# One encoder layer on one core: the state-space model's input operand built in its transposed layout

## The chip, the core and the metric

The kernel runs on one core of a Trainium2 chip. The metric is the device time of one execution in microseconds (us). The matrix engine is TensorE (PE in the rows; PEld is its weight load), the others are VectorE (DVE), ScalarE (ACT), GpSimd (POOL) and SyncE (SP), which issues every DMA of this kernel. The instructions of all engines are written out in a fixed order when the kernel is built; at run time each engine works through its own list and waits on semaphores.

## The reference

One layer of a streaming encoder, in float32: x is (512, 1024), 256 memory tokens, model width 1024.

```
z = rms_norm(x) @ w_in            # -> u (1024), q, k, v (1024 each), gates (2048)
a = S5(u): per group g of 64 (16 channels, 64 complex states):
    lam_bar = exp(lam * dt);  b_bar = (lam_bar - 1) / lam * b
    state_l = lam_bar * state_(l-1) + b_bar @ u_l          # over 512 positions
    y_l = Re(c @ state_l) + d * u_l
    a = gelu(y); a = a * sigmoid(a @ w_glu + b_glu); a = a @ w_ssm_proj
b = differential attention (8 heads, rotary, chunk-causal) @ w_da_proj
x = x + rms_norm((g_a * a + g_b * b) @ w_mix_out)
x = x + rms_norm(cross_attention(x, mem));  x = x + rms_norm(relu(x @ w_ff1)^2 @ w_ff2)
```

## The kernel before

**Wide products.** Every float32 product with a weight is done as three products in the reduced format fp32r: operand and weight are split into a high and a low part, and high*low, low*high and high*high are added up in PSUM. A weight unit is 128 x 1024 values. A DMA brings it (`wraw`, two buffers), ScalarE makes the high part (`whi`), VectorE or POOL the low one (`wlo`, four buffers). A projection (`proj`, L443) takes one unit and one PSUM bank and runs 24 products of 512 columns. The eight banks of PSUM are shared out by class with `quotas`: in the stretch of interest three for projections ("mm"), two for transposes and small products ("t"), two for attention scores ("s"), one for attention outputs ("o") (`QUO`, L71).

**Order.** The kernel is written as coroutines. `spawn` gives each a rank (the R values, L60), and a planner (`step`, L248) keeps for each engine the time up to which it is filled, by its own cost figures. It always lets the coroutine of lowest rank go on whose next instruction is ready: an instruction of another engine is written when TensorE's planned time has reached the time at which its inputs are ready, and at which its engine is filled for no more than `SLACK` (L56, 700 ns) ahead (`when`, L244). A DMA is written `SLACK` ahead of the time at which its source is ready (`load`, L228). The projections come in a fixed sequence from the `filler`, at the worst rank: first v, then for each head the u, q and k products and some gate products (`ULEAD` and `GL`, the number of gates behind each head). `self.X` writes an operation to VectorE or POOL, whichever the planner has done earlier; `self.Y` is VectorE alone while `YX` is 0. `PORT` says for each phase whether the planner keeps operations of the two that use a common port apart.

**Attention.** q and k of a head are rotated (`rope`, L938) in tiles `ropeB` and `ropeA`, of which there is one each, and moved by six DMAs a product into the operands. Four blocks a head compute scores, softmax, the difference of the two maps, a transpose and the output; `PBUF` (3) is the number of softmax buffers.

**State-space model.** The 64 groups are worked off in eight steps m of eight groups, four pairs each. Positions are cut into 64 chunks of 8; the powers of lam_bar are made once (`ssm_tables`, L664): `L` to the power 8, in float32, and `Lw` = powers times (lam_bar - 1)/lam, kept in SBUF; `L`, its imaginary part and the negative of that also go to DRAM (`scr_L`). Then for each m:

- `ssm_pre` (L764), rank 0.1: loads b and c (`bc`) and rows of the powers (`L2`); E = Lw x b (complex, six operations of 512 columns); copies E's first step into `bb`, block by block (four ScalarE copies); C = c x powers (three operations of 1024 columns and a copy).
- `ssm_mid` (L803): transposes E by eight TensorE transposes into two banks, and two ScalarE copies bring them to `ET`; the product of `bb` and C gives the kernel of short distances, which goes through DRAM (`sk`) and comes back as eight DMAs of 16 rows (`Dt`, one buffer).
- `ssm_main` (L847): waits for u of this m, loads it (`u2`), takes `ET` x u (state product, 32 small products), rotates back and forth around a scan over the chunks (`rr`, z, `S["s"]`), and adds C x state and `Dt` x u (64 small products) to y. GELU and four DMAs to DRAM follow.

The tiles `E`, `ET`, `bb`, the temporaries and z are cuts of one tile `ga`. After the eighth m, `gelu` (L1077) reads y back and splits it, and the GLU products begin; each needs all eight. The merge of the branches waits for the GLU and for all heads.

Of the kernel before, what the change touches and what calls it, by code (L numbers as in the profile page):

```python
# [26 lines left out]
KB = 8  # L27
# [28 lines left out]
SLACK = 700.0  # L56
PORT = (1,1,1,1,0,0,0,0)
PACE = 2.5
PEM = 500.0
R_TAB, R_PRE, R_ROT, R_MID, R_MAIN, R_U, R_ATT, R_BLK, R_ROPE, R_GATE, R_W = 1, 0.1, -0.55, -0.3, -0.6, -0.5, -0.45, 0, -0.45, 0, -0.3  # L60
# [3 lines left out]
YX = 0  # L64
# [38 lines left out]
class Kern:  # L103
# [464 lines left out]
    def consts(self):  # L568
# [12 lines left out]
        self.scr_L = [self.dram.tile([P, NPAIR, T + 1], F32, name=f"scr_L{i}") for i in range(3)]  # L581
        self.scr_g = [self.dram.tile([P, SEQ], F32, name=f"scr_g{m}") for m in range(16)]
# [65 lines left out]
    def ssm_alloc(self, pool):  # L648
        S = self.S
        S["Lw_re"], S["Lw_im"] = (self.t(pool, [P, NPAIR, T], x) for x in ("Lw_re", "Lw_im"))  # L650
        S["qa_re"], S["qa_im"], S["qb_re"], S["qb_im"] = (self.t(pool, [P, NPAIR, T], x) for x in ("qa_re", "qa_im", "qb_re", "qb_im"))
        S["r8"] = self.t(pool, [P, NPAIR], "r8")
        S["bb"] = self.t(pool, [P, 4, 2, 2, 16], "bb")
        S["s"] = self.t(pool, [P, 4, 2, NC], "st")
        S["K"] = self.t(pool, [P, NSLOT, 16], "kev")
        for k in ("bb", "s", "K"):
            self.nc.gpsimd.memset(S[k], 0.0)
# [6 lines left out]
    def ssm_tables(self):  # L664
# [49 lines left out]
        nL = self.tmp(N, T + 1)  # L714
        yield from self.A.activation(out=nL, in_=L_im[:, :N], func=AF.Copy, scale=-1.0)
        for i, x in enumerate((L_re[:, :N], L_im[:, :N], nL)):
            yield from self.load(self.scr_L[i], x)
# [10 lines left out]
        for h in range(2):  # L728
            c = slice(4 * h, 4 * h + 4)
            yield from self.cmul4(v, S["Lw_re"][:, :, c], S["Lw_im"][:, :, c], L_re[:, :N, c], L_im[:, :N, c],  # L730
                                  w_re.unsqueeze(2).broadcast_to((P, N, 4)), w_im.unsqueeze(2).broadcast_to((P, N, 4)),
                                  *[x[:, :N] for x in tt])
# [31 lines left out]
    def ssm_pre(self, pool, m):  # L764

        v, g, S = self.V, self.G, self.S
        bc = yield from self.alloc(pool, [P, 384], "bc")
        yield from self.load(bc, self.a["bc"][m])
        L2 = yield from self.alloc(pool, [P, 2, 2, 36], "L2")
        for i, h, x in ((0, 0, 0), (0, 1, 0), (1, 0, 2), (1, 1, 1)):  # L770
            yield from self.load(L2[64 * h:64 * h + 64, i],
                                 self.scr_L[x][:, 4 * m:4 * m + 4].rearrange("(a s) j t -> s a (j t)", a=2))
        sl = slice(4 * m, 4 * m + 4)
        b_re, b_im = (bc[:, 64 * i:64 * i + 64].rearrange("p (j h) -> p j h", j=4) for i in range(2))
        L_re, L_im = S["Lw_re"][:, sl].unsqueeze(3), S["Lw_im"][:, sl].unsqueeze(3)
        t1, t2 = (x.rearrange("p (j t h) -> p j t h", j=4, h=16) for x in S["ct"])
        yield from self.lock("E")
        E_re, E_im = (x.rearrange("p (j t h) -> p j t h", j=4, h=16) for x in S["E"])
        sh = (P, 4, T, 16)
        yield from self.cmul(S["eng_e"], E_re, E_im, L_re.broadcast_to(sh), L_im.broadcast_to(sh),  # L780
                             b_re.unsqueeze(2).broadcast_to(sh), b_im.unsqueeze(2).broadcast_to(sh), t1, t2)
        yield from self.lock("bb")
        for par in range(2):
            s = slice(64 * par, 64 * par + 64)
# [3 lines left out]
        sh = (P, 8, T, 16)  # L788
        x, y = (bc[:, 128 * i:128 * i + 128].rearrange("p (j h) -> p j h", j=8) for i in (1, 2))
# [472 lines left out]
    def build(self):  # L1262
# [116 lines left out]
        def rot_all():  # L1379
            for m in range(8):  # L1380
                yield from self.ssm_rot(sp, m)
# [299 lines left out]
```

## Time and profile before

| | us |
|---|---|
| median of 3 runs | 1077.8 (1073.1 to 1080.18) |
| profiled execution | 1077.05 |
| its span, first to last instruction | 1075.0 |
| TensorE busy | 1057.1 (98%) |
| VectorE busy | 645.1 (60%) |
| ScalarE busy | 525.9 (49%) |
| POOL busy | 71.8 (7%) |

The busy time of TensorE is modelled and a product overlaps the next, so a wide product shows 390 ns where the next begins some 227 ns after it. Starts are therefore what to compare. The stages are: v, tables and normalisation (to about 60 us), state-space model and attention (to about 362 us), GLU (to 416 us), merge and output projection, cross-attention (to about 730 us), MLP.

### The profile page before, as it was taken

The page shows a single profiled execution, that of the slowest core. Times are in us where ns is not written, and L with a number is a line of the kernel's source. Part 1 is how long each engine was busy: PE and PEld are TensorE (multiplying, and loading weights), DVE is VectorE, ACT ScalarE, POOL GpSimd, SP SyncE. Part 2 cuts the span into 40 slices and gives each one's busy share as a digit, 9 for nine tenths or more (in the row PEclk, how much of TensorE's full clock was granted, in tenths as well). Part 3 has the DMA queues.
Part 4 walks back from the last instruction along what each step waited for, and adds up shares of the span by engine and source line. Part 5 has one row for each costly group of instructions (what it writes and reads, how often), then busy time and mean ns, then how long its engine had stood idle before and what let it go on. Part 6 is the DMA issues. An engine that isn't in the chain of part 4 may idle for free.

```text
span 1075.0 us, 15625 instructions
## 1 busy us (share of the span) xinstructions
PE 1057.1 (98%) x5854; PEld 884.0 (82%) x5854; DVE 645.1 (60%) x1125; ACT 525.9 (49%) x1051; POOL 71.8 (7%) x83
## 2 busy tenths in 40 slices
PE   9999999999999999999999999999999999999997
PEld 7887788888887788888898888889888888888885
DVE  6898879988877774444487555475442223443234
ACT  6757567767766774222455444354342214433131
POOL 1020201010200000000022000010000000000001
PEclk9999999999999999999999999999999999999999
DMA  8458377585774954444565512323332333332322
GB/s 301 138 150 216 106 172 202 137 201 141 188 169 127 215 147 136 143 142 141 193 212 159 157 59 59 119 79 118 98 97 92 94 95 96 97 97 98 98 78 79
DMA packets 96042, 146.38 MB, mean 136 GB/s; under 512 B 45664, under 2 KB 57440, under 8 KB 95968
## 3 DMA queue, kind: packets, MB, share of 16 engines
q1 hardware_dynamic: 95968, 145.39, 46.5%
q8 instruction: 46, 0.75, 0.3%
q14 instruction: 28, 0.23, 0.1%
HBM read 120.87 MB, written 11.91 MB: 124 GB/s over the span
## 4 chain that ended last, share of the span: by engine, by line
PE 87%; DVE 5%; ACT 3%; DMA 2%; issue 2%; SPq 1%; POOL 0%; POOLq 0%; DVEq 0%; ACTq 0%
PE ps L368 85%; PE ps L377 2%; DVE wlo L98 1%; DVE ga L98 1%; ACT ropeB L98 1%; SPq L219 1%; DMA xr<-in_x_dram 1%; DMA q<-ropeB 1%; DMA scr_u<-ev 0%; DMA Dt<-sk 0%; DVE hTl L98 0%; ACT p L98 0%; ACT whi L98 0%; POOL ropeB L98 0%; DVE ropeA L98 0%
## 5 line engine op out<-in xcount | busy, mean ns | idle before, releaser
L98 DVE TENSOR_TENSOR wlo<-wraw,whi 128x1024 fp32r<-128x1024 f32 (+1 forms) x180 | 217.7, 1209 | 294.2 <-ACT whi L98 291.2
L98 ACT CAST whi<-wraw 128x1024 fp32r<-128x1024 f32 (+1 forms) x180 | 185.9, 1033 | 285.7 <-PE ps L368 257.3
L368 PE MATMUL ps<-hTl,whi 128*128 128x512 f32 (+1 forms) x736 | 286.9, 390 | 0.4 <-DVE sm L98 0.4
L368 PE MATMUL ps<-hTh,wlo 128*128 128x512 f32 (+1 forms) x736 | 280.7, 381 | 0.0
L368 PE MATMUL ps<-hTh,whi 128*128 128x512 f32 (+1 forms) x736 | 280.7, 381 | 0.0
L368 PEld LDWEIGHTS ps<-hTh,whi 128*128 128x128 f32 x736 | 138.7, 188 | 27.2
L368 PEld LDWEIGHTS ps<-hTl,whi 128*128 128x128 f32 x736 | 138.9, 189 | 25.1 <-issue 1.2
L368 PEld LDWEIGHTS ps<-hTh,wlo 128*128 128x128 f32 x736 | 139.0, 189 | 23.4
L368 PE MATMUL ps<-whi,vy 128*128 128x512 f32 x384 | 123.6, 389 | 0.0
L368 PE MATMUL ps<-whi,g2l 128*128 128x512 f32 x256 | 99.7, 389 | 0.0
L368 PE MATMUL ps<-wlo,vy 128*128 128x512 f32 x224 | 87.7, 392 | 0.0
L368 PEld LDWEIGHTS ps<-whi,vy 128*128 128x128 f32 x384 | 72.1, 188 | 15.0
L368 PE MATMUL ps<-wlo,g2h 128*128 128x512 f32 x192 | 74.9, 390 | 0.0
L368 PE MATMUL ps<-whi,g2h 128*128 128x512 f32 x192 | 74.7, 389 | 0.0
L368 PE MATMUL ps<-vy,whi 128*128 128x512 f32 (+1 forms) x256 | 65.4, 338 | 0.0
L368 PEld LDWEIGHTS ps<-whi,g2l 128*128 128x128 f32 x256 | 48.1, 188 | 9.8
L98 POOL TENSOR_TENSOR sm<-sm,mhalf 128x1 f32<-128x1 f32 (+1 forms) x28 | 26.3, 942 | 364.7 <-DVE sm L98 358.8
L368 PEld LDWEIGHTS ps<-wlo,vy 128*128 128x128 f32 x224 | 42.1, 188 | 8.5
L368 PEld LDWEIGHTS ps<-vy,whi 128*128 128x128 f32 x256 | 44.4, 189 | 5.0
L98 DVE TENSOR_REDUCE sm<-ps 128x1 f32<-128x256 f32 (+3 forms) x80 | 37.0, 472 | 15.2 <-PE ps L368 15.0
L368 PE MATMUL ps<-vy,wlo 128*128 128x512 f32 (+1 forms) x128 | 43.0, 336 | 0.0
L368 PEld LDWEIGHTS ps<-wlo,g2h 128*128 128x128 f32 x192 | 36.0, 188 | 7.6
(220 smaller groups left out, 1514.5 us busy)
## 6 DMA issues: line engine op xcount, KB each, us to landing
wraw<-in_wall_dram SPq DMA_DIRECT2D x172, 512.0 KB, 3.6
xr<-in_x_dram SPq DMA_DIRECT2D x8, 512.0 KB, 5.5
q<-ropeB SPq DMA_DIRECT2D x32, 128.0 KB, 3.4
scr_g<-gt SPq DMA_DIRECT2D x16, 256.0 KB, 4.4
Dt<-sk SPq DMA_DIRECT2D x64, 64.0 KB, 3.3
gl<-scr_g SPq DMA_DIRECT2D x16, 256.0 KB, 3.8
mg<-scr_y SPq DMA_DIRECT2D x12, 256.0 KB, 4.5
gain<-in_gains_dram SPq DMA_DIRECT2D x5, 512.0 KB, 5.4
```

What stands on the lines that cost most here:

```text
L98: getattr(k.eng[best], "copy" if (best, m) == ("ACT", "tensor_copy") else m)(**kw)
L219: self.nc.sync.dma_start(out=out, in_=in_)
L368: self.nc.tensor.matmul(out, lhsT=lhsT, rhs=rhs, start=start, stop=stop, **kw)
L377: self.nc.tensor.transpose(out, in_, self.ident)
```

## The change

E is no longer built in the layout of C and transposed. In the tables, the powers are transposed once (four TensorE transposes for all m) and stored in DRAM (`scr_W`); a new coroutine `ssm_in`, rank 0.1, loads for each m the rows of powers, each broadcast to 16 partitions by a DMA (`Lt`, eight DMAs), and b in the transposed layout from the host (`bt`), and computes `ET` directly with four operations. The factor (lam_bar - 1)/lam, which was in E, is now in C: `scr_L` holds Lw, its negative real part and its negative imaginary part, and C takes nine steps at once (1152 columns) without the copy. `bb` comes from the host within `bc`. The signs of the second half of the state are dropped, since C has them. With it, the constants of the planner are changed.

```
-SLACK = 700.0
-PORT = (1,1,1,1,0,0,0,0)
+SLACK = 1800.0
+PORT = (1,1,1,0,0,0,0,0)
-R_TAB, R_PRE, R_ROT, R_MID, R_MAIN, R_U, ... = 1, 0.1, -0.55, -0.3, -0.6, -0.5, ...
+R_IN = 0.1
+R_TAB, R_PRE, R_ROT, R_MID, R_MAIN, R_U, ... = 1, 0.1, -0.55, -0.3, -0.6, -0.7, ...
-YX = 0
+YX = 1
-GL = (1,2,3,3,3,2,1,1)
+GL = (1,1,1,1,2,2,4,4)
-QUO = dict(mm=3,t=2,s=2,o=1)
-PBUF = 3
-WTB = 2
+QUO = dict(mm=2,t=3,s=2,o=1)
+PBUF = 2
+WTB = 3
-R_X = -1.4
-R_XS = -0.2
+R_X = -0.6
+R_XS = -1.6
...
 # ssm_tables: powers to DRAM, transposed
+        Lc = S["bt"][:, 0].rearrange("p (x n) -> p x n", x=2)
+        for x, l in enumerate((L_re, L_im)):
+            yield from self.A.copy(out=Lc[:, x].rearrange("p (m t j) -> p m j t", t=T, j=4),
+                                   in_=l[:, :N, :T].rearrange("p (m j) t -> p m j t", j=4))
+        pt = yield from self.bank("t")
+        for x in range(2):
+            for i in range(2):
+                self.tr(pt[:, (2 * x + i) * P:(2 * x + i + 1) * P], Lc[:, x, i * P:(i + 1) * P])
+        Lt = S["bt"][:, 1]
+        yield from self.A.copy(out=Lt, in_=pt)
...
+        for h in range(3):      # Lw in cuts of bt, then to scr_L, negated by ScalarE
+            c = slice(3 * h, 3 * h + 3)
+            yield from self.cmul4(v, Lw[0][:, :, c], Lw[1][:, :, c], L_re[:, :N, c], L_im[:, :N, c], ...)
+        yield from self.load(self.scr_L[0], Lw[0])
+        for i in range(2):
+            nL = Lw[2 - i]
+            yield from self.A.activation(out=nL, in_=Lw[i], func=AF.Copy, scale=-1.0)
+            yield from self.load(self.scr_L[1 + i], nL)
...
 # ssm_pre: E, the copies into bb and the copy into C are gone
-        yield from self.cmul(S["eng_e"], E_re, E_im, L_re.broadcast_to(sh), L_im.broadcast_to(sh), ...)
-        for par in range(2):
-            yield from self.A.copy(out=S["bb"][:64, :, par, par], in_=E_re[s, :, 0])
-            yield from self.A.activation(out=S["bb"][64:, :, par, par], in_=E_im[s, :, 0], func=AF.Copy, scale=-1.0)
-        yield from self.A.copy(out=C[:, :, 0], in_=x)
+        yield from self.lock("ct")
+        yield from self.X.tensor_tensor(out=C, in0=lr, in1=x, op=ALU.mult)      # 1152 columns
+        yield from self.X.tensor_tensor(out=t3, in0=li, in1=y, op=ALU.mult)
+        yield from self.X.tensor_tensor(out=C, in0=C, in1=t3, op=ALU.add)
+        self.unlock("ct", t3)
...
+    def ssm_in(self, pool, m):
+        S = self.S
+        yield from self.load(S["bt"].rearrange("p x n -> p (x n)"), self.a["bt"][m])
+        for t in range(T):
+            yield from self.load(S["Lt"][16 * t:16 * t + 16].rearrange("h x n -> h (x n)"),
+                                 self.scr_W[m, t].rearrange("x j n -> (x j n)").partition_broadcast(16))
+        yield from self.lock("ET")
+        sh = (P, 2, 512)
+        Lt, bt, ET, t1 = S["Lt"], S["bt"], S["ET"], S["ct"]
+        yield from self.X.tensor_tensor(out=ET, in0=Lt[:, 0:1].broadcast_to(sh), in1=bt, op=ALU.mult)
+        yield from self.lock("ct")
+        yield from self.X.tensor_tensor(out=t1, in0=Lt[:, 1:2].broadcast_to(sh), in1=bt[:, ::-1], op=ALU.mult)
+        yield from self.X.tensor_tensor(out=ET[:, 0], in0=ET[:, 0], in1=t1[:, 0], op=ALU.subtract)
+        yield from self.X.tensor_tensor(out=ET[:, 1], in0=ET[:, 1], in1=t1[:, 1], op=ALU.add)
+        self.unlock("ct", t1)
+        (r8t: four ScalarE copies, moved here from ssm_pre)
...
 # ssm_mid: no transposes of E
-        for i, E in enumerate((E_re, E_im)):
-            pt = yield from self.bank("t")
-            for j in range(4):
-                self.tr(pt[:, j * P:(j + 1) * P], E[:, j].rearrange("p t h -> p (t h)"))
-            yield from self.A.copy(out=S["ET"][i]..., in_=pt...)
+        bb = bc[:, 256:].rearrange("p (j a b h) -> p j a b h", j=4, a=2, b=2)
```

## Rows read from the trace of the kernel before

**Rows 1.** Page, part 1: engine, busy us, share of the span, instructions.

```profile
PE 1057.1 (98%) x5854; PEld 884.0 (82%) x5854; DVE 645.1 (60%) x1125; ACT 525.9 (49%) x1051; POOL 71.8 (7%) x83
```

**Rows 2.** Busy time by stretch: PE, PEld, DVE, ACT, POOL, clock, DMA share, GB/s.

```profile
110.00:345.00 235.00, 230.56 (x1797) 190.53 (x1799) 199.81 (x374) 162.74 (x398) 26.23 (x20) 0.99 0.64 164
...
730.00:1040.00 310.00, 310.00 (x1413) 258.58 (x1412) 116.23 (x128) 103.71 (x138) 2.81 (x2) 1.00 0.32 99
```

**Rows 3.** TensorE's waits: total us, times, longest.

```profile
PE ps L368 <- DVE rr L98: 2.5, 1, 2.5
PE ps L368 <- ACT st L98: 1.7, 1, 1.7
PE ps L377 <- DVE xn L98: 1.7, 1, 1.7
```

**Rows 4.** Timeline of TensorE, 108 to 109 us: start, length, instruction.

```profile
108.42 0.60 PE L377 MATMUL ps<-ident,ga 128*128 128x128 f32 x4
...
108.85 0.38 PE L377 MATMUL ps<-ident,p 128*128 128x128 f32 x2
```

**Rows 5.** Instructions on the tile `ga`: count, ns min/median/max, first and last start.

```profile
L368 PE MATMUL ps<-u,ga x256: 222/222/271, 106.7 to 325.4; 128*64 128x64 f32 x128
...
L377 PE MATMUL ps<-ident,ga x64: 270/272/298, 84.4 to 306.0; 128*128 128x128 f32 x64
...
L98 ACT COPY bb<-ga x16: 235/243/249, 77.9 to 295.9; 64x64 f32<-64x64 f32 x16
...
L98 ACT COPY ga<-ps x16: 567/586/598, 89.0 to 307.6; 128x512 f32<-128x512 f32 x16
...
L98 DVE TENSOR_TENSOR ga<-Lw_re,bc x15: 674/685/695, 73.3 to 285.2; 128x512 f32<-128x512 f32 x15
...
L98 DVE TENSOR_TENSOR C<-C,ga x8: 1204/1222/1225, 83.9 to 303.4; 128x1024 f32<-128x1024 f32 x8
```

**Rows 6.** Timeline around the wait at 112 us.

```profile
111.00 1.28 DVE L98 TENSOR_TENSOR rr<-ps,R 128x512 f32<-128x512 f32 x2
...
112.42 0.67 PE L368 MATMUL ps<-C,bb 128*32 128x128 f32 x16 [2.53 <-DVE rr L98]
```

**Rows 7.** Stretches behind two waits; columns as in rows 2.

```profile
112.00:116.00 4.00, 3.58 (x27) 3.01 (x28) 3.97 (x9) 1.03 (x3) 0.00 (x0) 0.72 0.94 259
...
344.00:348.00 4.00, 3.81 (x66) 3.45 (x67) 3.02 (x5) 2.96 (x6) 0.00 (x0) 0.73 0.09 19
```

**Rows 8.** Timeline around the wait at 344 us.

```profile
341.26 2.34 ACT L98 COPY ropeB<-ps 32x512 f32<-32x512 f32 x4 [1.98 <-DMA q<-ropeB]
...
343.63 0.85 ACT L98 ACTIVATE st<-ga 64x252 f32<-64x252 f32 x2
...
344.09 0.76 PE L368 MATMUL ps<-st,C 128*64 128x64 f32 x4 [1.74 <-ACT st L98]
```

**Rows 9.** Timeline, 73 to 87 us: last products of k and gate 0, their evacuations.

```profile
73.30 0.39 PE L368 MATMUL ps<-hTh,whi 128*128 128x512 f32 x1
...
78.74 0.39 PE L368 MATMUL ps<-hTh,whi 128*128 128x512 f32 x1
...
81.53 0.69 ACT L98 ACTIVATE gt<-ps,hbg 128x512 f32<-128x512 f32 x1
...
86.50 0.69 DVE L98 TENSOR_TENSOR ropeA<-ps,cos 128x512 f32<-128x512 f32 x1 [1.39 <-ACT ropeB L98]
```

**Rows 10.** Timeline of SP, 132 us.

```profile
132.01 4.44 SPq L219 DMA_DIRECT2D Dt<-sk  x8
```

**Rows 11.** Timeline, the first GLU product.

```profile
363.12 0.47 PE L368 MATMUL ps<-g2l,whi 128*128 128x512 f32 x1 [0.59 <-issue]
```

**Rows 12.** Timeline, VectorE and POOL, 101 to 111 us.

```profile
101.05 1.22 DVE L98 TENSOR_TENSOR wlo<-wraw,whi 128x1024 fp32r<-128x1024 f32 x1
...
107.99 1.50 POOL L98 TENSOR_TENSOR ga<-Lw_im,bc 128x512 f32<-128x512 f32 x1
...
108.50 2.08 DVE L98 TENSOR_TENSOR wlo<-wraw,whi 128x1024 fp32r<-128x1024 f32 x1
109.46 1.60 POOL L98 TENSOR_TENSOR ga<-qa_re,qb_re 128x256 f32<-128x256 f32 x1
```

More of the change, by code (lines that the diff above doesn't have):

```diff
@@ L713, in ssm_tables @@
                                   *[x[:, :, :s] for x in tt])
[L714 to L717, printed above, removed]
+        Lc = S["bt"][:, 0].rearrange("p (x n) -> p x n", x=2)
[3 more added lines that the diff above has]
+        pt = yield from self.bank("t")
+        yield (None, self.rdy(Lc))
+        for x in range(2):
[3 more added lines that the diff above has]
+        yield from self.A.copy(out=Lt, in_=pt)
+        self.unbank(pt)
+        for x in range(2):
+            for i in range(2):
+                yield from self.load(self.scr_W[4 * i:4 * i + 4, :, x].rearrange("m t j n -> (m t) j n"), Lt[:, (2 * x + i) * P:(2 * x + i + 1) * P])
         x1, x2 = self.tmp(N), self.tmp(N)
@@ L727, in ssm_tables @@
         yield from self.cmul4(v, w_re, w_im, x1, L_im[:, :N, 1], aa, x2, *t0)
[L728 to L732, printed above, removed]
+        cut = S["bt"].rearrange("p x n -> p (x n)")
+        Lw = [cut[:, 288 * i:288 * i + 288].rearrange("p (j t) -> p j t", j=N) for i in range(3)]
+        for h in range(3):
+            c = slice(3 * h, 3 * h + 3)
+            yield from self.cmul4(v, Lw[0][:, :, c], Lw[1][:, :, c], L_re[:, :N, c], L_im[:, :N, c],
+                                  w_re.unsqueeze(2).broadcast_to((P, N, 3)), w_im.unsqueeze(2).broadcast_to((P, N, 3)),
+                                  *[x[:, :N, :3] for x in tt])
+        yield from self.load(self.scr_L[0], Lw[0])
+        for i in range(2):
+            nL = Lw[2 - i]
+            yield from self.A.activation(out=nL, in_=Lw[i], func=AF.Copy, scale=-1.0)
+            yield from self.load(self.scr_L[1 + i], nL)
         r8 = S["r8"]
@@ L791, in ssm_pre @@
         t3 = S["ct2"].rearrange("p (j t h) -> p j t h", j=8, h=16)
-        yield from self.A.copy(out=C[:, :, 0], in_=x)
-        yield from self.X.tensor_tensor(out=C[:, :, 1:], in0=lr, in1=x.unsqueeze(2).broadcast_to(sh), op=ALU.mult)
-        yield from self.X.tensor_tensor(out=t3, in0=li, in1=y.unsqueeze(2).broadcast_to(sh), op=ALU.mult)
-        yield from self.X.tensor_tensor(out=C[:, :, 1:], in0=C[:, :, 1:], in1=t3, op=ALU.add)
-        C = C.rearrange("p (a j) t h -> p j a t h", a=2)
-        self.drop(bc, L2)
+        yield from self.lock("ct")
@@ L848, in ssm_main @@
         v, S = self.V, self.S
-        C, r8t, Dt = S["m", m]
-        while ("u", m) not in S or ("R", m) not in S:
-            yield lambda: ("u", m) in S and ("R", m) in S
+        C, Dt = S["m", m]
+        while any((x, m) not in S for x in "uRE"):
+            yield lambda: all((x, m) in S for x in "uRE")
+        r8t = S["E", m]
         u2 = yield from self.alloc(pool, [P, 8, NC], "u2")
@@ L855, in ssm_main @@
         e4 = ep.rearrange("p (i j c) -> p i j c", i=2, j=4)
[L856 to L857 removed]
+        ET = S["ET"].rearrange("p i (j n) -> p i j n", j=4)
+        yield (None, self.rdy(u2, ET))
         for j in range(4):
@@ L886, in ssm_main @@
             for par in range(2):
-                yield from self.A.activation(out=S["s"][half[i], :, par, 1:], in_=jc(z)[half[par], :, :n], func=AF.Copy,
-                                             scale=-1.0 if i else 1.0)
+                yield from self.A.copy(out=S["s"][half[i], :, par, 1:], in_=jc(z)[half[par], :, :n])
         self.drop(R4)
@@ L1377, in ssm_all, with in_all @@
                 yield from self.ssm_pre(sp, m)
+        def in_all():
+            for m in range(8):
+                yield from self.ssm_in(sp, m)
         def rot_all():
```

75 lines of the change are left out of this document (33 added, 42 removed).

## The prediction

> **What bounds the kernel now.** I read the engine totals first, then the same totals by stretch, then the list of what TensorE waited for, and last the order of time around each of those waits. The totals put TensorE at 98% of the span [rows 1]. By stretch it is filled completely where the MLP runs (310.0 of 310 us, VectorE 116); in the stretch of the state-space model and the attention, 110 to 345 us, it is busy 230.6 of 235 us while VectorE is busy 199.8 and ScalarE 162.7 [rows 2]. So a microsecond of TensorE work taken out of that stretch comes off the end, a microsecond of VectorE or ScalarE work does not, unless TensorE waits for it. The waits are few: 2.5 us for VectorE's `rr`, 1.7 us for ScalarE's `st`, 1.7 us for `xn` [rows 3]. After the first two, the granted clock was 0.72 and 0.73 of full in a stretch of 4 us [rows 7], where it had been 1.00: part of that stretch ran at the lower level (1.2 of 2.4 GHz), which lost 4 x 0.28 = 1.1 us and, with the 2 us behind it, I take 1.7 us for each.
>
> **Transposes.** The change takes out the transposes of E. There are 64 of them [rows 5]; four in a row begin at 108.42 and the next instruction begins at 108.85 [rows 4], so four cost TensorE 0.43 us. 16 groups x 0.43 = 6.9 us go; the tables get one group of four, +0.4. Net **-6.5 us**, on the path, as TensorE is full there.
>
> **Work of the other engines, for each of the 8 groups m.** Out: six VectorE operations of 512 (0.69 us each, 4.1 us), four copies into `bb` (0.24 us), two evacuations of 0.59 us, one copy into C. In: two operations of 1024 (1.22 us, the price of a C operation of that size), two of 512, and C's three operations grow by an eighth (+0.15 us each) [rows 5]: 4.3 us. VectorE stays as it was; ScalarE loses about 2.4 us x 8 = 19 us. Both lie under TensorE, **0**; without that cover the VectorE part would cost 8 x 0.2 = 1.6 us. In the tables, the narrower pieces, two copies, an evacuation, and stores that wait for each other through `bt` add a few us, beside the v, u, q and k products; 0, and at most those few us in the start of group 0, which now waits for the C operations alone and no longer for E's 4.1 us ahead of them.
>
> **DMAs.** SP issues nine more DMAs for each m (`bt`, eight rows of `Lt`). Eight `Dt` issues behind a wait took 4.4 us [rows 10], so SP spends about 5 us more in each round of 31 us. What is queued behind them on SP are the weights, the q and k moves and the `Dt` and `u2` loads of the next group. Bounds: 0 when they fall in the gap after the state product, where ET becomes free, and 8 x 5 = 40 us when they stand before `Dt` each time. Their place is near the state product; the first of those ran at 106.7 and the `Dt` loads behind it at 132.0 [rows 5, 10], 25 us later, which is nearest to the first end: **0**. In bytes it is 8 x 1.06 = 8.5 MB; the DMA engines moved 164 GB/s at a busy share of 0.64 [rows 2], at which 8.5 MB are 33 us of the 235: the share goes to about 0.78, still not full.
>
> **The wait of 2.5 us.** The product `C,bb` waited at 112.42 for VectorE's reading of a bank (`rr<-ps`, to 112.28) [rows 6]: the small-product class "t" had two banks and both were held. The change gives it three, so this wait and its slow clock go: **-4.2 us**; bounds 0 (the bank is taken by something else) and -4.2. Late next are the `Dt` rows, which come 20 us later and are not waited for.
>
> **The wait of 1.7 us** for `st` came from ScalarE's own order: four copies into `ropeB`, 2.34 us, stood before `st`, and the product stood first in TensorE's queue [rows 8]. Nothing in the change forbids it; ScalarE is lighter. Bounds 0 and -3.4; I take **0**. The wait for `xn` lies in a stretch that only the larger SLACK touches: 0, bounds +-1.7.
>
> **Banks of the projections.** "mm" goes from three to two. This is the term that can turn the sign. A k projection ended at 73.69 and its bank was read last by `ropeA<-ps` at 87.19, because q's rotation has to leave the single `ropeB` first; the gate after it ended at 79.13 and was evacuated at 82.22 [rows 9]. With three banks the next projection began at once; with two it begins when the gate's bank is free, 3.1 us later, unless small products fill the gap. Bounds: 0, and 8 heads x 3.1 = 25 us. To fill it there are the small products of attention and model: 1797 products ran in the 235 us, where 1413 x 235/310 = 1071 wide ones would fit [rows 2], so some 700 and more are small; only in the first head is there no attention to fill with. I take one full gap, **+3 us**, the end near which the seven other heads lie.
>
> **The last heads.** Gates are moved behind heads 6 and 7 (four each), away from heads 1 to 5. In the kernel before the last q and k products stand close together, and the gate product stops at the GLU with a wait of 0.6 us for the last GELU [rows 11]; more filler there covers the model's last group as the fill gets 6.5 us shorter. 0. PBUF 2 leaves two attention blocks in flight, behind the same cover; WTB 3, PORT and the R values only reorder work that is under TensorE: 0.
>
> **POOL.** YX lets the 16 rotations back (`rr<-rr,R` and z) run on POOL. While POOL multiplied from 107.99 to 111.06, VectorE's `wlo` took 2.08 us and not 1.22 [rows 12]: 0.86 us lost. By that, 32 such operations on POOL would cost VectorE at most 28 us against about 18 us that it is spared (16 x (0.69 + 0.42)), in a stretch where it has 35 us left: 0 in the sum. The Trainium skill's "SBUF — State Buffer", section "Who interferes with whom", speaks against this edit: a VectorE instruction with two SBUF inputs and a GpSimd one that reads SBUF exclude each other, the later one standing still for the whole of the other. The trace agrees in kind (2.08 us); by the page the sum would be the same, as long as VectorE stays hidden.
>
> **Sum.** -6.5 - 4.2 + 3 = -7.7. The profiled execution took 1077.05 us (span 1075.0 and 2.05 around it), so 1069.4; it lies 0.75 below the median of 1077.8. Predicted: **1069.4 us**, 0.8% under the median. A change of 1%, 10.8 us, is what can be told from none here: under 1067.0 is faster, over 1088.6 slower. With the bounds of the nearest terms (-3.4 to the one side, +6.5 when the bank term doubles and the `rr` wait stays partly) the forecast's own range is 1063 to 1076. Chance 0.50, a third of it under 1067.
>
> **Rival 1, all waits go.** Larger SLACK and a lighter ScalarE also clear the `st` wait with its clock and the `xn` wait, and small products fill every bank gap: -6.5 - 4.2 - 3.4 - 1.7 = -15.8, 1061. For it: these waits are misjudged orders, not missing throughput. Against: every new order can bring its own. 0.22.
>
> **Rival 2, two banks are too few (slower).** The place is behind each k projection, the price 3.1 us for a head that has nothing to fill it. It decides from an average of 10.7/8 = 1.3 us a head, where the transposes and the `rr` wait are eaten up; at full price 1077.05 - 6.5 - 4.2 + 25 = 1091. For it: k's bank was held 13.5 us in the quietest head. Against: attention and the model. 0.18, half of it over 1088.6.
>
> **Rival 3, the model's round gets longer.** Its eight state products run from 106.7 to 325.4 [rows 5], one each 31.2 us, a serial loop: `Dt` loads behind the last product, `u2`, state product, some eight dependent VectorE and ScalarE steps, product. SLACK is the depth to which an engine is filled with lower ranks; 1.1 us more of it ahead of each step is 8 x 1.1 x 7 = 62 us at worst, some 15 us of which the moved gates and the left attention cover: about 1077 - 6.5 + 47 = 1117. It decides from 0.3 us a step (15/56). Against: VectorE has 15% left, so the depth is seldom full, and YX gives the loop a second engine. 0.08, most of it slower. That the nine new DMAs lengthen the same round is counted here.
>
> The other 0.02 is that E's transposes were hidden in other waits and nothing moves: 1077.
>
> **Numbers.** Faster: 0.50/3 + 0.22 = 0.38, of which I leave 0.01 to the middle: 0.37. Slower: 0.09 + 0.06 = 0.15. Within: 0.48. The range leaves out the lower edge of rival 1 and the far parts of rivals 2 and 3: 1058 to 1089.
>
> **What would show it.** No transposes of `ga` and 8 x 8 broadcasts of `Lt`; TensorE busy some 6 us less up to 416 us; no wait before `C,bc`. Rival 2 shows as idle TensorE before projections whose first instruction follows a gate's or u's evacuation; rival 3 as state products more than 31 us apart and a long wait for `g2l` before the GLU. The prediction is wrong if the projections stay dense and the time is still over 1076, or if the waits shift to places that the list of before doesn't have.

## The result, and the profile after

The changed kernel takes **1088.5 us** (1087.23 to 1088.74, 4 runs) against 1075.5 us, ratio 1.0119 with the interval 1.0095 to 1.0142. It is 1.2% slower; the forecast was 1069.4 us. The profiled execution took 1087.23 us, its span is 1085.5.

Part 1 of the page (engine, busy us, share of the span, instructions) answers to [rows 1]:

```profile
PE 1055.1 (97%) x5794; PEld 878.4 (81%) x5794; DVE 648.8 (60%) x1113; ACT 511.4 (47%) x999; POOL 74.8 (7%) x84
```

TensorE does 60 instructions less, and its share falls from 98% to 97%. Busy time by stretch of the kernel after (columns as in [rows 2]) shows where:

```profile
110.00:345.00 235.00, 225.42 (x1739) 185.10 (x1739) 208.38 (x378) 159.35 (x393) 37.12 (x27) 0.99 0.73 192
345.00:430.00 85.00, 81.35 (x471) 66.29 (x470) 51.46 (x91) 51.19 (x110) 2.01 (x2) 1.00 0.63 161
...
730.00:1040.00 310.00, 309.46 (x1448) 259.49 (x1447) 120.81 (x138) 105.33 (x144) 4.92 (x4) 1.00 0.32 100
```

The kernel before, in the stretch that [rows 2] leaves out:

```profile
345.00:430.00 85.00, 84.32 (x464) 70.46 (x463) 53.41 (x97) 55.45 (x131) 4.30 (x4) 0.98 0.65 161
```

In 110 to 345 us TensorE is busy 225.4 of 235 us where it was 230.6 [rows 2], in 345 to 430 us 81.4 of 85 where it was 84.3. The MLP is as full as before but for half a microsecond. VectorE has 8.6 us more and ScalarE 3.4 us less than in [rows 2], neither full. So TensorE has less to do and waits more. The longest of its waits (total us, times, longest) answer to [rows 3]:

```profile
PE ps L378 <- DVE xn L99: 3.6, 2, 3.1
PE ps L369 <- DMA kh<-ropeB: 3.4, 5, 1.7
PE ps L369 <- ACT wt L99: 2.2, 3, 1.2
PE ps L369 <- ACT whi L99: 1.7, 1, 1.7
PE ps L369 <- DMA u<-scr_u: 1.5, 2, 0.9
PE ps L378 <- POOL mhalf L577: 1.4, 1, 1.4
PE ps L378 <- DVE p L99: 1.4, 1, 1.4
PE ps L369 <- DVE C L99: 1.1, 1, 1.1
```

The two waits for `rr` and `st` in [rows 3] are gone, and in their place stands a list of many short ones with different releasers: key moves (the DMAs that bring a head's rotated k into its operands), weights (`wt`, `whi`), u, softmax (`p`), C. No engine heads the list. From 60 to 376 us the timeline marks 17 waits of TensorE, and none of them stands before a projection: each stands before a product of the attention or of the state-space model. The wait for `xn`, 1.7 us before, is now 3.1 us; e8 will show where that comes from.

To count all of it I give each product the steady distance to the next start that its shape has in the trace (227 ns for 512 columns, 173 for 384, 120 for 256, 108 for 128 and for a transpose, 33 to 37 for the small ones) and call the sum the **floor**; what the starts lie further apart is the **excess** (my sums over the trace; it holds waits, the slow clock behind them, pipeline ends). Before: floor 1040.0, excess 25.8. After: floor 1033.5, excess 42.7. The floor fell by the 6.5 us of the 60 transposes; the excess rose by 16.9, and 16 us of that lie before 400 us or at the `xn` wait near 583 us.

One of the new waits at close range, timeline of TensorE (start, length, instruction, idle before it and its releaser):

```profile
103.93 0.40 PE L369 MATMUL ps<-hTh,whi 128*128 128x512 f32 x1
106.06 0.30 PE L369 MATMUL ps<-k,q 128*128 128x128 f32 x1 [1.74 <-ACT whi L99]
...
107.83 0.45 PE L369 MATMUL ps<-k,q 128*128 128x128 f32 x1 [0.91 <-DMA k<-ropeA]
...
109.37 0.63 PE L369 MATMUL ps<-hTh,wlo 128*128 128x512 f32 x1
109.79 0.63 PE L369 MATMUL ps<-hTh,whi 128*128 128x512 f32 x1
```

Busy time and clock around this wait and the `xn` wait (columns as in [rows 2]):

```profile
104.00:112.00 8.00, 5.36 (x19) 4.13 (x18) 3.97 (x9) 4.79 (x12) 0.00 (x0) 0.79 0.84 168
582.00:592.00 10.00, 6.93 (x32) 5.79 (x32) 7.32 (x9) 4.87 (x9) 1.45 (x2) 0.83 0.56 164
```

The first attention products of a head begin 2.1 us after the projection before them, wait again for a key move, and the wide products behind start 0.42 us apart in place of 0.23: the granted clock was 0.79 of full in these 8 us and 0.83 around the `xn` wait, so part of each stretch ran at the lower level, 1.2 GHz. The list names ScalarE's `whi` for the first of the two waits, though `whi` is no operand of that product. Whether it was `whi` or a key move, both hang on DMAs that stood behind the same loads on SP:

```profile
93.41 0.33 SPq L220 DMA_DIRECT2D sk<-kev  x1
93.79 0.43 SPq L220 DMA_DIRECT2D bt<-in_bt_dram  x1
94.66 3.98 SPq L220 DMA_DIRECT2D ga<-scr_W  x8
...
99.84 0.51 SPq L220 DMA_DIRECT2D k<-ropeB  x1
...
103.64 6.08 SPq L220 DMA_DIRECT2D Dt<-sk  x8
```

`bt` and the eight rows of `Lt` took SP from 93.8 to 98.6 us, behind them came the key moves (from 99.84), and only then the eight `Dt` loads, which took 6.1 us. The `wraw` load of that `whi` was issued at 99.22. The instructions on the tile `ga` answer to [rows 5] (count, ns min/median/max, first and last start):

```profile
L369 PE MATMUL ps<-u,ga x256: 222/222/271, 114.2 to 347.8; 128*64 128x64 f32 x128
...
L220 SPq DMA_DIRECT2D ga<-scr_W x64: 302/418/490, 74.6 to 304.3; - x64
...
L99 DVE TENSOR_TENSOR ga<-rr x16: 407/420/427, 126.6 to 359.9; 128x256 f32<-128x256 f32 x16
...
L99 DVE TENSOR_TENSOR ga<-ga,bt x10: 1211/1216/1869, 83.2 to 323.4; 128x1024 f32<-128x1024 f32 x10
...
L99 POOL TENSOR_TENSOR ga<-ga,bt x6: 2364/2394/2647, 115.5 to 319.3; 128x1024 f32<-128x1024 f32 x6
```

The first state product runs at 114.2 us (106.7 in [rows 5]), the last at 347.8 (325.4). Six of the sixteen products with `bt` went to POOL at 2.39 us in place of 1.22 us on VectorE; the sixteen rotations back that YX would let run there (`ga<-rr`) all stayed on VectorE.

### The profile page after: what moved, and what is told of

The parts are those of the page before. It is cut to its first block, busy times and chain, and to the rows that moved or that the text cites. A ratio compares the mean times of both kernels' runs of the same rounds, so it can differ in the third digit from the quotient of the medians.

```text
span 1085.5 us, 15557 instructions
## 1 busy us (share of the span) xinstructions
PE 1055.1 (97%) x5794; PEld 878.4 (81%) x5794; DVE 648.8 (60%) x1113; ACT 511.4 (47%) x999; POOL 74.8 (7%) x84
## 4 chain that ended last, share of the span: by engine, by line
PE 83%; DVE 5%; DMA 5%; ACT 3%; SPq 2%; issue 2%; POOL 0%; POOLq 0%; DVEq 0%; ACTq 0%
PE ps L369 81%; SPq L220 2%; PE ps L378 2%; DMA kh<-ropeB 1%; DVE ga L99 1%; DVE wlo L99 1%; DMA wraw<-in_wall_dram 1%; ACT ropeB L99 1%; DVE rr L99 1%; ACT whi L99 1%; DMA xr<-in_x_dram 1%; DMA q<-ropeB 1%; DVE sm L99 1%; DMA k<-ropeA 0%; DMA bt<-in_bt_dram 0%
## 5 line engine op out<-in xcount | busy, mean ns | idle before, releaser
L369 PEld LDWEIGHTS ps<-hTh,wlo 128*128 128x128 f32 x736 | 139.1, 189 | 23.6
L99 ACT COPY ropeB<-ps 32x512 f32<-32x512 f32 x64 | 37.0, 578 | 14.7 <-DMA kh<-ropeB 5.8
L99 DVE TENSOR_REDUCE sm<-ps 128x1 f32<-128x128 f32 (+3 forms) x80 | 36.4, 469 | 11.1 <-PE ps L369 10.9
```

Of the source, the lines that this page charges most:

```text
L99: getattr(k.eng[best], "copy" if (best, m) == ("ACT", "tensor_copy") else m)(**kw)
L369: self.nc.tensor.matmul(out, lhsT=lhsT, rhs=rhs, start=start, stop=stop, **kw)
```

## The experiments

The theories. **B**: one of the smaller buffers is the price (banks for the projections, softmax buffers). **P**: the new path is slower by itself, as its nine loads and its late start hold up the model's groups. **O**: no part is; the planner builds the whole order anew for every edit, the order of the kernel before was an unusually dense one, and the change got a looser one. Each ratio is to the kernel before as it ran beside that run, so a difference of medians between rows can be off by a microsecond or so. Floor is 1040.0 us for each kernel with the old path and 1033.5 for each with the new one; excess is that of the profiled run.

| run | path | median us | ratio to before, interval | excess |
|---|---|---|---|---|
| before | old | 1075.5 | | 25.8 |
| after | new | 1088.5 | 1.0119, 1.0095 to 1.0142 | 42.7 |
| e1 | new | 1104.2 | 1.0259, 1.0223 to 1.0295 | 61.3 |
| e2 | old | 1092.2 | 1.0156, 1.0118 to 1.0193 | 38.2 |
| e3 | new | 1091.5 | 1.0142, 1.0114 to 1.0171 | 47.1 |
| e4 | old | 1090.4 | 1.0136, 1.0103 to 1.0168 | 38.0 |
| e5 | new | 1098.4 | 1.0219, 1.0191 to 1.0247 | 53.4 |
| e6 | new | 1096.1 | 1.0192, 1.0172 to 1.0212 | 50.1 |
| e7 | new | 1089.0 | 1.0128, 1.0099 to 1.0157 | 45.6 |
| e8 | old | 1089.2 | 1.0130, 1.0098 to 1.0162 | 38.6 |
| e9 | new | 1084.9 | 1.0087, 1.0071 to 1.0103 | 40.2 |
| e10 | old | 1074.8 | 0.9983, 0.9970 to 0.9996 | 23.6 |
| e11 | new | 1118.1 | 1.0386, 1.0369 to 1.0404 | 76.4 |
| e12 | new | 1097.6 | 1.0212, 1.0184 to 1.0240 | 58.4 |
| e13 | new | 1070.1 | 0.9957, 0.9945 to 0.9970 | 25.4 |
| e14 | new | 1076.3 | 1.0011, 1.0002 to 1.0020 | 31.1 |
| e15 | old | 1074.3 | 0.9992, 0.9982 to 1.0001 | 23.4 |
| e16 | new | **1065.9** | 0.9910, 0.9896 to 0.9924 | 21.3 |
| e17 | new | 1076.6 | 1.0007, 0.9988 to 1.0026 | 26.6 |
| e18 | new | 1086.3 | 1.0103, 1.0088 to 1.0118 | 41.2 |

**E1: the changed kernel with three projection banks.**

```
-QUO = dict(mm=2,t=3,s=2,o=1)
+QUO = dict(mm=3,t=2,s=2,o=1)
```

> The changed kernel with three banks for projections and two for small products again (QUO as before), all else as changed. Theory A (two banks are too few: q and k hold both while the rotation of the head before is under way, and TensorE has no projection to run): the waits behind k projections go, some 13 to 17 us come back, 1072 to 1076 us. Theory B (the constants as a set make the heads come faster than the rotation and the attention can take them, so that a third bank is held as well): within 6 us of the changed kernel, 1083 to 1095 us, with idle TensorE between projections still there.

It got 15.6 us slower, outside both forecasts. Read by itself that speaks against a lack of banks; e8 will show why it can't be read by itself.

**E2: the old path with every new constant** (SLACK, PORT, R_U, YX, GL, QUO, PBUF, WTB, R_X, R_XS).

```
-SLACK = 700.0
+SLACK = 1800.0
...
-R_XS = -0.2
+R_XS = -1.6
```

> The kernel before (E built and transposed) with all planner constants of the change. If the constants alone cost the time: about 1075 + 13 + 6.5 = 1090 to 1096 us, since the transposes stay. If the new path for ET (nine more DMAs for each m, ET built on the critical loop) costs it: near the kernel before, 1072 to 1080 us.

1092.2 us: without the new path the constants cost 16.6 us.

**E3: the new path with the old constants**, but for PBUF 2, which its tables leave room for.

```
-SLACK = 1800.0
+SLACK = 700.0
...
-R_XS = -1.6
+R_XS = -0.2
```

> The new path for ET with the planner constants of before, but for PBUF, which stays at 2 because three softmax buffers don't fit beside bt. If the constants cost the time: 1069 us, 6.5 us under the kernel before. If the new path does: 1085 to 1090 us. If two softmax buffers do: as much over 1069 us as the next kernel is over 1075.

1091.5 us, just above the band for the path: the path without the constants costs as much. The two don't add up: together they cost 13.

**E4: the kernel before with two softmax buffers.**

```
-PBUF = 3
+PBUF = 2
```

> The kernel before with PBUF 2 and nothing else changed. If two softmax buffers slow the heads so much that projections run out: 1083 to 1092 us, with idle TensorE near the end of the attention stretch, 300 to 400 us. If attention is under other work: 1073 to 1079 us.

1090.4 us, and TensorE runs dry in the last heads, at a clock of 0.91. It looked like the cause (theory B); e8 and e16 put it in doubt. Busy time by stretch, e4:

```profile
345.00:430.00 85.00, 73.57 (x363) 61.32 (x361) 52.20 (x101) 57.09 (x139) 6.89 (x6) 0.91 0.63 152
```

**E5: the new path with all old constants.** The second half of `rr` stands in `rsb`, which leaves room for three softmax buffers.

```
-S["rr"] = [self.t(sp, [P, 2, 256], f"rr{i}") for i in range(2)]
+S["rr"] = [self.t(sp, [P, 2, 256], "rr0"), self.rsb.rearrange("p (i n) -> p i n", i=2)]
...
-PBUF = 2
+PBUF = 3
```

> The new path alone, with every constant of the kernel before, three softmax buffers among them; the room for its tables comes from letting the second half of rr stand in rsb, a tile that lives in the same stretch anyway. Theory B (the two softmax buffers cost the time, as the 14.8 us that they cost the kernel before would say): the 6.5 us of the transposes are gained, about 1069 us, ratio 0.99 to 1.0, heads' on transposes ending near 415 us. Theory P (the path itself starts the state-space model late, because its tables take a longer way through DRAM and eight more loads stand ahead of Dt in SP's queue, and the gated linear unit then waits for the last group): 1082 to 1092 us, ratio 1.006 to 1.016, last y product 10 us or more after the 347.3 us of before and TensorE waiting for g2l behind it. Theory O (the order of before is an unusually dense one, and any other order gives some of it back): 1080 to 1090 us, with small waits spread over 100 to 400 us, no single cause.

1098.4 us where theory B had 1069: with three softmax buffers it is slower still, and 6 us above the highest of the three forecasts (theory P, up to 1092). 31.8 of its 53.4 us of excess lie in 300 to 400 us, where the clock fell with the waits (0.88 of full from 345 to 430 us).

**E6: the same with early tables.**

```
-R_TAB, ... = 1, ...
+R_TAB, ... = -0.4, ...
```

> As the run before it, with the tables' rank at -0.4 in place of 1, so that their work goes ahead of other work of the start. Theory P: the late start is most of the loss, so the first state product comes 8 us or more earlier than in the run before it and the time falls by 6 to 12 us, to 1075 to 1083 us. Theory B: no change, 1069 us in both. Theory O: no change within 4 us, 1080 to 1090 us in both, wherever the group's start goes.

The first state product came 9.1 us earlier (114.0 in place of 123.1), the time fell by 2.2 us. That is the small difference that theory O expected, at a time (1096.1) that no theory had. The order was planned anew, so the 2.2 us are no clean price of the start; e18 gives a better one.

**E7: the same, the nine loads made for group 0 alone.**

```
+if m == 0:
     yield from self.load(S["bt"]...)
-for t in range(T):
+for t in range(T if m == 0 else 0):
```

> As the run before it, but the nine loads for the operand (bt and the eight of Lt) are made for group 0 alone; the groups after it use group 0's tables, so the output is of other data and the instructions of the engines are the same. Theory P, with the nine loads in SP's queue as its second part: 6 to 12 us less than the run before it, 1066 to 1073 us. If the loads are hidden: within 3 us of the run before it. Theory O: 1078 to 1088 us.

7.1 us less, inside what theory P expected of the difference (its time, 1066 to 1073 us, was missed by 16). But the order was planned anew as well; e18 separates the two.

**E8: the kernel before with another SLACK and nothing else.**

```
-SLACK = 700.0
+SLACK = 1800.0
```

> The kernel before, with SLACK 1800 in place of 700 and nothing else (one of the change's constants): the same instructions on the same tiles in another order. Theory O: 1081 to 1090 us, ratio 1.005 to 1.014, as the order of before is hard to match. Theories P and B have nothing that acts here: 1073 to 1079 us, ratio 0.998 to 1.003.

1089.2 us. The same instructions on the same tiles, in another order (the planner put 7 of VectorE's operations on POOL and 2 of POOL's on VectorE), cost 13.6 us, as much as the whole change. Theory O takes the lead here: a kernel whose order is changed by anything can lose this much, so no single edit that is planned anew, e4's included, prices what it edits. Busy time by stretch, e8:

```profile
110.00:345.00 235.00, 230.92 (x1843) 190.19 (x1842) 197.92 (x364) 161.06 (x395) 29.54 (x24) 0.99 0.60 157
345.00:430.00 85.00, 79.41 (x393) 65.33 (x392) 52.22 (x100) 56.75 (x136) 7.18 (x6) 0.98 0.69 173
```

One of TensorE's waits, e8:

```profile
PE ps L377 <- DVE xn L98: 3.8, 2, 3.2
```

SLACK is one of the change's own constants, though, and a part of its price is no matter of chance. The longest wait for `xn`, near 585 to 605 us there, is 3.1 to 3.2 us in all five kernels with SLACK 1800 (after, e1, e2, e8, e18), on both paths, and at most 2.0 in every other (e12, with 2000 and a searched order, has the 2.0). With the slow clock behind it, the excess at this place is 1.9 us before, 4.6 after and 5.0 in e8. So some 3 us of e8's 13.6, and as many of the change's loss, go with SLACK 1800 itself; the rest of e8's loss is spread over other waits. Apart from PBUF (e4), no second constant was turned by itself in the kernel before.

**E9 to E12: searched orders, and one load of `Lt`.** The ranks and other constants of the planner (SLACK, BX, BW, YX, GL, ULEAD, R_X and R_XS) were varied at random, and those with the earliest end by the kernel's own planner were run, for the new path (e9, e12) and the old (e10). In e9, e11 and e12 one DMA fetches all of `Lt`; e9 also has the hold, by which a group's loads wait for the `Dt` loads of the group before. The edit of e11 against e6, and the hold:

```
-for t in range(T):
-    yield from self.load(S["Lt"][16 * t:16 * t + 16]..., self.scr_W[m, t]....partition_broadcast(16))
+yield from self.load(S["Lt"]..., self.scr_W[m]....unsqueeze(1).broadcast_to((T, 16, 1024)))
...
+while m > 0 and ("m", m - 1) not in S:
+    yield lambda: ("m", m - 1) in S
```

> The new path with three softmax buffers, its eight loads of Lt made as one DMA of the same bytes, ssm_in of a group held until the group before it has issued its Dt loads, early tables, and ranks, BX, BW and GL picked anew (by the end that the kernel's own planner gives) for the densest order. Theory O (the change lost its 6.5 us because the order planned for it is looser than that of before): with an order as dense as that of before the gain shows, excess over steady spacing near 26 us, 1064 to 1073 us, ratio 0.990 to 0.998. Theory P (the path is slower by itself, through its loads and its late start): 1080 us or more whatever the order.

> The kernel before with ranks picked in the same way and with as many trials. Theory O: the order of before was already about the best of its path, so 1070 to 1079 us, ratio 0.996 to 1.003; if ranks alone could give more, 1066 us or less, and then e9's gain would not be the path's. Theory P has nothing that acts here.

> As the run with early tables (1096.1 us), but the eight loads of Lt are one DMA of the same bytes. If the eight issues in SP's queue were what the nine loads cost (7.1 us), 1088 to 1091 us; if it was their bytes, 1094 to 1098 us. Theory O alone: anything from 1085 to 1098 us, by the order that comes out.

> The new path with one load of Lt as in e9, without the hold, and with a second set of ranks, BX, BW, GL and ULEAD, picked in the same way from another start. Theory O: as dense an order by another way, 1066 to 1076 us, ratio 0.991 to 1.001. Theory P: 1080 us or more. If e9 gains and this one does not, the hold is what the path needs.

E10 stayed within 0.2% of before: the search found little on the old path. E9 and e12 missed the forecasts of theory O and came out over 1080 us, as theory P had it. E11 looks for a reason in the single load: with it the kernel is 22.0 us slower than e6, outside every forecast, though its order was planned anew too. SP's issues for group 2, timeline of e6:

```profile
127.74 0.53 SPq L220 DMA_DIRECT2D bt<-in_bt_dram  x1
128.32 5.68 SPq L220 DMA_DIRECT2D ga<-scr_W  x8
```

The same of e11:

```profile
136.35 0.38 SPq L220 DMA_DIRECT2D bt<-in_bt_dram  x1
136.79 0.65 SPq L220 DMA_DIRECT2D ga<-scr_W  x1
```

The key moves in e6's list of DMA issues (last number: median us from issue to landing):

```profile
k<-ropeB SPq DMA_DIRECT2D x16, 128.0 KB, 4.1
```

And in e11's:

```profile
k<-ropeB SPq DMA_DIRECT2D x16, 128.0 KB, 9.9
...
kh<-ropeB SPq DMA_DIRECT2D x16, 128.0 KB, 8.1
```

And in e9's, where the hold is added:

```profile
k<-ropeB SPq DMA_DIRECT2D x16, 128.0 KB, 2.8
```

SP is done with the rows of `Lt` in 0.65 us and not in 5.7, but the key moves, issued behind them, land after 8 to 10 us and not some 4. Five of TensorE's waits in e11, of 2.9 to 4.1 us each and 16.9 us together, stand before the first `k,q` product of a head, which needs these moves (three of them are marked as for a key move); in e6 no wait for a key move is over 0.6 us. In e12, which has the single load and no hold, the moves land after 4.4 to 9.3 us. So without the hold the eight loads are the better form, and e12 says little on the theories. In e9 the moves land after 2.4 to 3.3 us; its 1084.9 us have another reason, which stays open, and it counts as a miss of theory O. The packet count on e6's page:

```profile
DMA packets 99819, 155.56 MB, mean 142 GB/s; under 512 B 46880, under 2 KB 58144, under 8 KB 99744
```

And on e11's:

```profile
DMA packets 98858, 155.55 MB, mean 139 GB/s; under 512 B 45920, under 2 KB 57184, under 8 KB 98784
```

The packets under 512 B fell by 960, which is 64 loads with 16 each against 8 loads with 8 each (1024 - 64). The Trainium skill ("DMA: Bandwidth & Descriptors", section "Rules for kernel authors") says that a DMA whose outermost dimension has fewer than 16 entries runs on no more than that many of the 16 engines; the single load's has 8, and the count agrees. A single load with another dimension outermost was not tried.

**E13 to E15: searched orders again, the new path with its own eight loads** (e13 and e14 with the hold, three softmax buffers and three projection banks; the planner counts SP's issue at 600 ns in e13 and e15).

```
-self.free["SP"] = st + 60
+self.free["SP"] = st + 600
```

> As e9, but with the change's own eight loads of Lt (e11 showed that the single load holds up the key moves behind it: 9 to 11 us to landing against 2 to 6 us), and with ranks, BX, BW and GL picked again, SP's issue taken at 600 ns in the planner in place of 60 (the trace has 0.3 to 0.6 us for one). Theory O: 1066 to 1076 us, ratio 0.990 to 1.000, excess over steady spacing 25 to 30 us. Theory P: no better than e9's 1085 us, as the path holds its own waits in any order.

> The new path with its eight loads and the hold, with another set of ranks, BX, BW, GL and ULEAD, planned with SP's issue at 60 ns as in the kernel before. Theory O: 1070 to 1080 us. If SP's issue time in the planner is what the new path lacks, e13 comes out 8 us or more below this one. Theory P: 1085 us or more.

> The kernel before with the planner's SP issue at 600 ns and ranks, BX, BW, GL and ULEAD picked in the same way as e13's. Theory O: near e10, 1070 to 1078 us. If the 600 ns makes better orders by itself, 1062 to 1069 us, and the gain of e13, if any, is not the path's alone.

E13 takes 1070.1 us with 25.4 us of excess, the excess of the kernel before, and is faster than it by 0.3 to 0.55%: on an order as dense as the old one the 6.5 us of the transposes are there (4.9 us by the medians; 6.7 us by the profiled spans, 1068.3 against 1075.0, but the profiled execution of before lay 1.6 us above its median). E14 has 6 us more excess and lies 0.1% above before. That is 6.2 us by the medians where 8 were asked for to blame the planner's 60 ns, and e15 shows that the 600 ns give the old path nothing; that question stays open. Theory P, which had 1085 us in any order, falls, for a path that has the hold: no kernel with the eight loads and a searched order was run without it.

**E16 and E17: one of the change's two splits put back into e13**, each with an order picked for it.

```
e16: -PBUF = 3, WTB = 2         +PBUF = 2, WTB = 3
e17: -QUO = dict(mm=3,t=2,...)  +QUO = dict(mm=2,t=3,...)
```

> The new path of e13 with PBUF 2 and WTB 3 as in the change, mm 3 and t 2 as in e13, and ranks, BX, BW, GL and ULEAD picked again for it. If two softmax buffers cost nothing by themselves (the 14.8 us of e4 were its order): 1064 to 1074 us, ratio 0.989 to 0.999. If they cost what e4 measured: 1080 us or more in any order.

> The new path of e13 with the change's bank split (mm 2, t 3) and three softmax buffers, ranks and the rest picked again for it. If two banks for the projections are the price (Rival 2 of the prediction): 1076 to 1090 us, 6 us or more above e13, with gaps between projections where both banks wait for their evacuations. If banks are neutral and e1's 15.6 us were its order: 1066 to 1076 us.

E16 is the fastest kernel of all, 0.9% below before, with the change's two softmax buffers. Busy time by stretch, e16:

```profile
110.00:345.00 235.00, 234.42 (x1802) 194.99 (x1802) 208.32 (x377) 163.32 (x399) 21.62 (x21) 1.00 0.77 201
345.00:430.00 85.00, 85.00 (x415) 71.36 (x414) 50.18 (x87) 49.02 (x104) 6.36 (x5) 1.00 0.65 171
...
730.00:1040.00 310.00, 310.00 (x1370) 256.69 (x1370) 20.02 (x13) 99.83 (x133) 207.69 (x115) 1.00 0.31 97
```

TensorE's longest waits, e16:

```profile
PE ps L369 <- DVE wlo L99: 3.1, 1, 3.1
PE ps L369 <- DVE C L99: 1.5, 1, 1.5
PE ps L378 <- POOL mhalf L577: 1.4, 1, 1.4
PE ps L378 <- DVE xn L99: 1.3, 4, 0.5
```

TensorE is busy 234.4 of 235 us and then 85.0 of 85, where the changed kernel had 225.4 and 81.4, with the same path and the same VectorE time (208.3 and 208.4 us). The waits of over half a microsecond that are left lie before 75 us and after 500 us. E17 is 6.5 us above e13 by the medians (5.4 by the ratios), at intervals that don't meet, and so just inside the band that was given for a price of two banks; but its runs spread from 1071.2 to 1083.5, and its profiled run, the fastest, has e13's excess (26.6). Two projection banks cost something between nothing and some 6 us; the size stays open.

**E18: the changed kernel, order held, without the later loads.** The planner counts the loads of groups 1 to 7, and nothing is issued for them.

```
-self.nc.sync.dma_start(out=out, in_=in_)
+if real: self.nc.sync.dma_start(out=out, in_=in_)
...
-yield from self.load(S["bt"]..., self.a["bt"][m])
+yield from self.load(S["bt"]..., self.a["bt"][m], real=m == 0)
```

> The changed kernel with every engine's order as it is, but bt and the eight parts of Lt are fetched for group 0 alone: the planner counts the loads of groups 1 to 7 and nothing is issued for them, so the groups after 0 use group 0's tables and the output is of other data. This prices the nine loads with the order held fixed. If they are the path's own cost (Theory P): 1078 to 1083 us, 6 to 10 us below the changed kernel. If e7's 7.1 us were its order: 1086 to 1090 us, within 2 us of the changed kernel.

Busy time by stretch, e18:

```profile
110.00:345.00 235.00, 223.07 (x1719) 184.22 (x1716) 209.82 (x376) 159.09 (x387) 37.48 (x27) 0.99 0.61 162
```

Three of TensorE's waits, e18:

```profile
PE ps L378 <- DVE p L99: 4.7, 2, 3.4
...
PE ps L369 <- DMA u<-scr_u: 2.7, 2, 1.4
...
PE ps L369 <- DMA kh<-ropeB: 1.1, 2, 0.9
```

The first attention products of the head that waited at 106.06 us in the change, and the state products, e18:

```profile
104.16 0.22 PE L369 MATMUL ps<-k,q 128*128 128x128 f32 x1
```

```profile
L369 PE MATMUL ps<-u,ga x256: 222/222/316, 109.3 to 345.8; 128*64 128x64 f32 x128
```

2.2 us less (1.7 by the ratios), at intervals that overlap. Every engine has the change's instructions in the change's order; only the 63 loads are gone. The key moves are issued at 95.69 us in place of 99.84, the two waits behind them (106.06 and 107.83 us) are gone, and the first state product runs 4.9 us earlier. At the last state product 2.0 us of that are left and at the end of the span 1.3: later waits took the rest. The DMA share falls from 0.73 to 0.61 and the waits for `kh<-ropeB` from 3.4 to 1.1 us, others take their place (`p` 4.7 for 1.4). The loads cost at most a few microseconds of the 17; the rest of e7's 7.1 us I put down to its order, without a run that shows it.

## Why the prediction was wrong

**What failed** is a clause of *The last heads*: "WTB 3, PORT and the R values only reorder work that is under TensorE: 0", with the sum built on it. The sum took the waits of before as a list that stands but for the entries that the change touches. But ranks, SLACK, quotas and costs feed a planner that orders every engine anew, and the waits moved to places that the list of before doesn't have, which is the last of the signs that the prediction gave for being wrong: the excess rose by 16.9 us. Reordering alone cost 13.6 us (e8). By e8 and e4 the term should have been 0 to some 15 us, nearly all on one side, as e10 and e15, the best orders found for the old path, are no more than 0.3% below before. *Rival 1* had the argument ("every new order can bring its own") and used it only to lower a chance.

Step by step:
- **Transposes**, -6.5: right. 60 instructions at 108 ns went from TensorE, and e13, at the same excess, is 4.9 to 6.7 us faster than before.
- **The wait of 2.5 us**, -4.2, and **of 1.7 us**, 0: both waits went, and the excess rose all the same. A wait that goes is a gain only while the rest of the order stands.
- **The wait for `xn`**, 0 with the bounds +-1.7: the place was named rightly, the size was not: wherever SLACK is 1800 the longest such wait grew by 1.4 us or so, and with the slow clock behind it the cost is some 3, over the bound.
- **Banks of the projections**, +3: e17 leaves 0 to some 6. *Rival 2* gave 1091 us, close to the result, but its sign is missing: no wait of TensorE between 60 and 376 us stands before a projection. The near hit is luck; two banks can have acted only through the order planned for them. They were not tried in another order together with two softmax buffers.
- **PBUF 2**, 0: right as far as e16 goes, against e4's look; e16 has it and is the fastest.
- **DMAs**, 0 with the bounds 0 and 40: 2.2 us by e18. Where they would stand was wrong: in each of groups 1 to 7 they were issued ahead of the `Dt` loads of the group before (for group 1 at 93.8 against 103.6 us). That is the end of the bounds at which the sum had 40 us, and its price there was wrong too.
- **Work of other engines**: group 0 began 7.5 us later than before, and not "those few us"; 4.9 us of that went with the loads of group 1 (e18), and of these 1.3 were left at the end.
- *Rival 3* had the model's rounds as the bound. They did get longer, (347.8 - 114.2)/7 = 33.4 us in the change; but in e16 they are (317.5 - 93.3)/7 = 32.0 us, longer than the 31.2 of before, in a kernel that is 10 us faster. They don't bound it. Nor did the larger SLACK lengthen them: in e8 they are (323.5 - 108.5)/7 = 30.7 us.
- **POOL**, 0: not tested. The planner put none of the sixteen rotations on POOL, so what the term weighs did not happen, and e13 to e17 have YX 0. What POOL took were six products with `bt`, and VectorE is held up by them: a product with `bt` on VectorE that began within one on POOL took 1.87 us (1.22 in the median), 0.65 us more at an overlap of 0.79:

```profile
256.43 2.36 POOL L99 TENSOR_TENSOR ga<-ga,bt 128x1024 f32<-128x1024 f32 x1
...
258.00 1.87 DVE L99 TENSOR_TENSOR ga<-ga,bt 128x1024 f32<-128x1024 f32 x1
```

  The Trainium skill says so ("SBUF — State Buffer", section "Who interferes with whom"), and the trace agrees in kind.

**The cause, as far as shown:** the change does save what it says, and lost 17 us with the order that came with it. The same path, in e16 with the same softmax buffers, runs 22.7 us faster than the changed kernel in another order, and the old path loses 13 to 15 us in another order (e8; e4 with one buffer less besides). Of the 17 us, nearly 3 are the wait for `xn`, which goes with SLACK 1800, and about 2 the later loads (e18); the rest is spread over waits of at most 1.4 us each, with the slow clock behind them. **Open:** which setting makes the changed kernel's order loose. Between it and e16 lie the bank split, the hold, the `rr` room, YX, the planner's 600 ns and some twenty constants, and only the bank split was put back by itself, with three softmax buffers. Every kernel of the new path under 1080 us has the hold, the `rr` room and YX 0, so no run tells what each of these gives. Six searched orders were run for the new path and two for the old one, so the best of the old is less well known.

## What to carry to other kernels

Where a planner or a list scheduler sets the order, an edit's price is what it takes from the bound engine plus the price of a new order; measure the second by turning constants that change no instruction in the kernel before, ahead of any forecast, and more than one, as each can have a price of its own (SLACK's 3 us). To price a part, hold the order fixed and leave out only that part; to judge a path, let each path have its own best order. Here a list of three waits over 1.5 us on an engine that was 98% full belonged to an order with more to lose (13.6 us) than to gain (0.3% at most by two searches).

## What the runs showed of the hardware

- One DMA that repeats eight rows 16 times each (512 KB), in place of eight that repeat one row each, let the key moves issued behind it land after 8.1 to 9.9 us in place of 3.6 to 4.1 (e11 against e6), and TensorE's waits before the products that need these moves came to 16.9 us. The kernels differ by 22.0 us, but also in order.
- Seven megabytes less (155.6 to 148.2 MB), nearly all in a stretch with a DMA share of 0.73, gave 2.2 us with the order held (e18): at that share the DMA engines were not what bounded the kernel.
- In e16 POOL made most of the MLP's splits (115 instructions, 207.7 us, VectorE 20.0), and TensorE stayed full at 310.0 us.
